# Mixer projections and gates as single fp32 products of unsplit weights

## The chip, the cores and the metric

The kernel runs on one core of a Trainium2 chip. The metric is the device time of one execution in microseconds (us). One execution is also recorded by the hardware profiler, with every instruction on its engine: PE (TensorE, the matmuls; PEld are its weight loads), DVE (VectorE), ACT (ScalarE), POOL (GpSimd) and SP, which issues most DMA transfers from one queue in order.

## The reference

Two layers of a diffusion transformer block on 256 context and 256 latent tokens, each token a vector of 1024. All is in fp32. The part around the change is the mixer: one normed input `h` is projected by one wide weight into the inputs of three mixers and a gate for each, and the gated outputs are merged.

```python
for layer in range(DEPTH):                       # DEPTH = 2
    x = ffn_half(x, ...); ctx = ffn_half(ctx, ...)
    h  = norm_modulate(x, ...);  hc = norm_modulate(ctx, ...)
    mix, mix_c = hybrid_mixer(h, hc, not last, w_in[layer], ...)
    x = x + m[5] * mix
    x = ffn_half(x, ...)                         # the context too, unless last

def hybrid_mixer(h, hc, need_ctx_out, w_in, ...):
    proj = h @ w_in                              # and proj_c = hc @ w_in
    u, k, v, f = split_cols(proj[..., :CTX_STATE_COLS], sizes)
    q = proj[..., CTX_STATE_COLS:MIX_COLS]
    y_s5  = s5_mixer(u, ...)                     # state space model, two directions
    y_att = gqa_mixer(q, k, v, ...)              # attention over context and latent
    y_rw  = rwkv7_mixer(f, ...)                  # RWKV-7 recurrence, two directions
    g_s5, g_att, g_rw = split(sigmoid(proj[..., MIX_COLS:]), 3)
    return (g_s5*(y_s5 @ w_br_s5) + g_att*(y_att @ w_br_att) + g_rw*(y_rw @ w_br_rwkv)) @ w_out
```

In the last layer only the latent tokens need an output, so the gates, the queries and some of `f` are computed for 256 tokens there.

## The kernel before

Activations lie with features on the partitions, as tiles of [128, 8, 512]: 8 blocks of 128 features by 512 tokens. A product of one 128x128 weight block with 256 tokens is called a product of 256 columns below; a [128x1024] strip of weights is 8 such blocks.

Precision is kept by splitting: `wsplit` (L904) copies an fp32 weight tile to a float32r tile `hi` on ACT (L906) and subtracts it on DVE or POOL (L907) to get `lo`; the FFN has its own `wunit` (L909). The norm writes its output split too, into `K.hhi` and `K.hlo` (`norm`, L1066). `mm3` (L921) then adds three float32r matmuls into one bank: hi by hi, hi by lo, lo by hi.

`mixers` (L1245) emits one layer's mixers. First the entry: two strips of RWKV's features (`pf` of t = 2, 3). Then `kknorm`, whose first matmuls write `kkss` (L110). Then the operations named in `SEQ`, in that order: `f` strips of RWKV's features (`pf`), `u` strips of S5's input (`pu`), `k` key/values (`pkv`), `q` queries (`pq`), `g4` or `g8` gates (`pg`). Those behind the bar are emitted inside `rw.run(between)`, between the two directions of the first half of RWKV's tokens. The rest of the 24 gates follow the attention. RWKV's own chain is: `prep`, which for each half of the tokens, direction and part computes `ZL`, `BK` and on PE `it` (L208), masked into `AM`; `solve_a`, which stores `AM` in DRAM (`Ad`), loads its diagonal blocks as `G`, inverts them in 15 short steps on DVE (`stmp` L240, `S` L241), and moves `S` through DRAM (`Sd`) into `D`; `solve_b`, which transposes `D` to `T` (DVE, L252) and starts the matmuls `pv` (L256); then the loop over chunks. S5 and attention (units of `atp`, `atP`, `ato`; L869 to L885) are emitted behind; then the merge: products `pb` with the gates, and `po` with `w_out`.

Code order is not engine order: the Tile framework's scheduler orders each engine's instructions when the kernel is built, from its own estimates and priorities; on the chip each engine runs its list in order and waits by semaphores. Weight tiles come from pools with few buffers: `wr` (3 of 256 KB), `gh` and `gl` (2 halves each) in the mixers.

Of the kernel before, what the change touches and what calls it, by code (L numbers as in the profile page):

```python
# [928 lines left out]
def dense(K,name,src,hhi,hlo,n0,nk=8,eng=None,alt=False,fill=False,cut=False,half=False,big=False):  # L929

    ps=mm(K,name,alt=alt); m=K.FM[n0>0]
    if cut: prods(K,ps,name,src,nk,hhi,hlo,n0,eng,half,big=big)
    else:
        for k in range(nk):
            j=slice(k%4*128,k%4*128+128)
            if k%4==0: hi,lo=wunit(K,src[:,k*128:(k+4)*128],512,eng)
            K.lastp=mm3(K.nc,ps[:,n0:],hi[:,j],lo[:,j],hhi[:,k,n0:],hlo[:,k,n0:],k==0,k==nk-1)
    return ps
# [14 lines left out]
def prods(K,ps,name,src,nk,hhi,hlo,n0,eng=None,half=False,z=512,big=False):  # L953

    w=K.NG if half else z-n0
    if big:
        for k in range(nk):
            if k%4==0:
                raw=K.rw.tile([128,512],F32,name=f"wr{name}{k}",tag="g2",bufs=K.TB[3])
                sp=K.rw.tile([128,2,512],F32R,name=f"wp{name}{k}",tag="f4",bufs=K.TB[0])  # L960
                K.nc.sync.dma_start(raw,src[:,k*128:k*128+512])
                wsplit(K,sp[:,0],sp[:,1],raw,eng)
            j=slice(k%4*128,k%4*128+128)
            for c in range(n0,z,w):
# [101 lines left out]
def norm(K,L,sub,n0,tag):  # L1066
# [24 lines left out]
    for h,v,s in hv:  # L1091
        for k in range(8):
          with K.tc.high_priority(offset=K.NQ) if v and n0==0 else nullcontext():
# [4 lines left out]
              if k%K.NP==K.NP-1:  # L1098
# [58 lines left out]
def build(tc,I,O,depth=DEPTH):  # L1157
    K=NS(); K.nc=nc=tc.nc; DQ=0; K.dq=nc.scalar if DQ&1 else nc.sync; K.S5C=2; K.FO=(6,0,1); K.FO2=(4,5,7); K.KV=0; K.FA=((),()); K.RG=2; K.EB=(); K.UP=(4,1); K.sq=nc.scalar if DQ&2 else nc.sync; K.rq=nc.scalar if DQ&4 else nc.sync; K.I=I; K.BG=(12,12); K.PO=4; K.SM=2; K.NPR=75; K.NQ=0; K.ATP=(1,1); K.GQ=((4,0),(0,0)); K.KP=9; K.PW=0; K.CA=6; K.NP=3; K.nu=0; K.after=None; K.hold=None; K.ADR=3; K.WB=3; K.TB=(4,4,10,4,4); K.ATT=3; K.ATQ=2; K.GA=(10,20); K.GB=(3,2); K.S5B=3; K.S5U=K.S5B; K.S5T=6; K.ATB=(2,1,1,1); K.fin=False; K.GTB=1; K.QB=(2,2); K.SP=2; K.GHB=2; K.NG=256; K.GP=2; K.HW=0; K.ORD='s s s s s g10 k u g3 u g3 u g3 u;s s s s s g20 k u g2 u'.replace('_',' ').split(';'); K.tc=tc; K.hop=None; K.FM=(6,9); K.GF=(24,24); K.HP=(5000,5000); K.HS=(0,0); K.HK=(0,0); K.ATT=5
# [9 lines left out]
    with es:  # L1168
# [9 lines left out]
        K.hhi=K.hp.tile([128,8,512],F32R,name="hhi"); K.hlo=K.hp.tile([128,8,512],F32R,name="hlo")  # L1178
# [63 lines left out]
v='v'  # L1242
def ix(v,L): return v[L] if isinstance(v,tuple) else v['v']

def mixers(tc,K,L,last):  # L1245
# [12 lines left out]
    with tc.tile_pool(name="mc",bufs=1) as mc, tc.tile_pool(name="q0",bufs=1) as q0, tc.tile_pool(name="prm",bufs=1) as K.prm, \  # L1258
# [194 lines left out]
```

## Time and profile before

| | |
|---|---|
| device time, median of 3 runs | 2347.73 us (2344.19 to 2353.74) |
| profiled execution: its own time / its span | 2359.33 us / 2357.6 us |
| mean granted clock of TensorE | 0.953 |
| PE, DVE, ACT, POOL busy | 95%, 69%, 41%, 26% |
| layer 0: `kkss`, first `pv`, second batch of `pv`, `po` | 466.8, 641.6, 724.0, 950.0 us |
| layer 1: the same | 1768.3, 1919.5, 1980.5, 2121.4 us |

The span is the time from the first to the last instruction in the trace. Busy time counts an engine's instructions with their overlaps taken out; a matmul's record is longer than the distance to the next one, since matmuls are pipelined. The last two lines are read from the starts of those instructions in the trace; they cut each layer's mixers into the three stretches that the prediction works with.

### The profile page before, as it was taken

Reading aid. Unit: us, or ns where it says so; the run is one execution under the profiler, and the core shown is the slowest. Engines: PE = TensorE matmul, PEld = TensorE weight load, DVE = VectorE, ACT = ScalarE, POOL = GpSimd, SP = SyncE. Lnnn points to the kernel's source line nnn. Section 1 sums busy time; section 2 is a strip of 40 time slices with the busy share of each in tenths; the row PEclk is TensorE's granted clock in tenths of the full one; section 3 lists DMA queues with packets and bytes.
Section 4 is the critical chain, followed back from the end, with each engine's and each line's share of the span. In section 5 each row is a group of like instructions: output and inputs, shape, how many; then the busy total and the mean of one; then the engine's idle time right before and its main releaser. Section 6 shows DMA issues by size and latency. Waiting matters only on the chain.

```text
span 2357.6 us, 40039 instructions
## 1 busy us (share of the span) xinstructions
PE 2242.8 (95%) x14438; PEld 1929.4 (82%) x14438; DVE 1623.2 (69%) x3202; ACT 973.7 (41%) x2005; POOL 607.1 (26%) x726
## 2 busy tenths in 40 slices
PE   7999889988999999899999999999999899998999
PEld 3888668866789889788888888888887688888999
DVE  7895889588855677886457575546557965687655
ACT  4333333433344544443233344334334325565554
POOL 5016660155422233600000002513013533331000
PEclk8999989998869999999999999999999877999999
DMA  7575566334422454545445436546424542365664
GB/s 254 165 225 171 182 214 219 121 119 144 123 82 76 138 163 143 185 141 184 123 143 182 126 131 206 171 155 215 138 65 131 150 126 85 94 194 184 178 188 130
DMA packets 222715, 363.40 MB, mean 154 GB/s; under 512 B 53554, under 2 KB 93618, under 8 KB 222388
## 3 DMA queue, kind: packets, MB, share of 16 engines
q1 hardware_dynamic: 220500, 360.09, 48.3%
q8 instruction: 113, 1.85, 0.3%
q10 hardware_dynamic: 2016, 0.76, 0.1%
q14 instruction: 86, 0.70, 0.1%
HBM read 320.90 MB, written 39.86 MB: 153 GB/s over the span
## 4 chain that ended last, share of the span: by engine, by line
PE 79%; DVE 10%; issue 4%; DMA 3%; POOL 2%; ACT 1%; SPq 1%; DVEq 0%; ACTq 0%; POOLq 0%
PE p L922 17%; PE p L924 17%; PE p L923 16%; PE pg L924 3%; PE pg L922 3%; PE pg L923 3%; DVE s L995 1%; PE pS L261 1%; PE pv L256 1%; PE pq L923 1%; PE po L922 1%; PE po L924 1%; PE po L923 1%; PE pq L922 1%; PE it L208 1%
## 5 line engine op out<-in xcount | busy, mean ns | idle before, releaser
L917 ACT ACTIVATE wh<-wr 128x512 fp32r<-128x512 f32 (+1 forms) x568 | 348.1, 619 | 666.3 <-PE p L923 578.1
L918 DVE TENSOR_TENSOR wl<-wr,wh 128x512 fp32r<-128x512 f32 (+1 forms) x568 | 407.3, 721 | 306.3 <-ACT wh L917 275.1
L922 PE MATMUL p<-hhi,wh 128*128 128x512 f32 (+1 forms) x1440 | 516.6, 363 | 4.7 <-ACT wh L917 3.6
L923 PE MATMUL p<-hlo,wh 128*128 128x512 f32 (+1 forms) x1440 | 518.6, 361 | 1.5 <-DVE hlo L1104 0.9
L924 PE MATMUL p<-hhi,wl 128*128 128x512 f32 (+1 forms) x1440 | 518.6, 361 | 0.6 <-DVE wl L918 0.6
L922 PEld LDWEIGHTS p<-hhi,wh 128*128 128x128 f32 x1440 | 273.2, 191 | 46.7 <-ACT wh L917 4.3
L923 PEld LDWEIGHTS p<-hlo,wh 128*128 128x128 f32 x1440 | 274.2, 190 | 42.9 <-DVE hlo L1104 1.8
L924 PEld LDWEIGHTS p<-hhi,wl 128*128 128x128 f32 x1440 | 274.0, 190 | 42.4 <-DVE wl L918 1.4
L995 DVE SCALAR_TENSOR_TENSOR s<-ad,cb 128x1024 f32<-128x1024 f32 x224 | 286.3, 1280 | 2.9
L924 PE MATMUL p<-ghi,wl 128*128 128x512 f32 (+1 forms) x704 | 248.3, 353 | 0.0
L922 PE MATMUL p<-ghi,wh 128*128 128x512 f32 (+1 forms) x704 | 248.0, 353 | 0.0
L923 PE MATMUL p<-glo,wh 128*128 128x512 f32 (+1 forms) x704 | 247.9, 353 | 0.0
L924 PE MATMUL pg<-hhi,glpg 128*128 128x256 f32 x512 | 157.9, 309 | 11.0 <-DVE glpg L907 9.0
L922 PE MATMUL pg<-hhi,ghpg 128*128 128x256 f32 x512 | 155.5, 304 | 0.3 <-ACT ghpg L906 0.3
L923 PE MATMUL pg<-hlo,ghpg 128*128 128x256 f32 x512 | 152.0, 297 | 0.0
L924 PEld LDWEIGHTS p<-ghi,wl 128*128 128x128 f32 x704 | 133.0, 189 | 18.2 <-issue 0.2
L923 PEld LDWEIGHTS p<-glo,wh 128*128 128x128 f32 x704 | 133.0, 189 | 18.1
L922 PEld LDWEIGHTS p<-ghi,wh 128*128 128x128 f32 x704 | 133.0, 189 | 17.9
L906 ACT ACTIVATE ghpg<-wrpg 128x256 fp32r<-128x256 f32 x176 | 72.3, 414 | 125.3 <-PE pg L923 102.9
L924 PEld LDWEIGHTS pg<-hhi,glpg 128*128 128x128 f32 x512 | 104.6, 205 | 18.8 <-DVE glpg L907 10.9
L907 POOL TENSOR_TENSOR glpg<-wrpg,ghpg 128x256 fp32r<-128x256 f32 x88 | 70.8, 808 | 180.8 <-ACT ghpg L906 168.7
L922 PEld LDWEIGHTS pg<-hhi,ghpg 128*128 128x128 f32 x512 | 104.8, 205 | 6.3 <-ACT ghpg L906 0.5
(722 smaller groups left out, 4325.5 us busy)
## 6 DMA issues: line engine op xcount, KB each, us to landing
wr<-w SPq DMA_DIRECT2D x480, 256.0 KB
ad<-w_ada SPq DMA_DIRECT2D x138, 512.0 KB
wrpg<-w_g SPq DMA_DIRECT2D x96, 256.0 KB
wr<-w SPq DMA_DIRECT2D x64, 192.0 KB
s5tab<-s5tabd SPq DMA_DIRECT2D x16, 640.0 KB
s5tabd<-s5tb SPq DMA_DIRECT2D x16, 384.0 KB
wrpf<-w_f SPq DMA_DIRECT2D x24, 256.0 KB
gd<-gt SPq DMA_DIRECT2D x24, 256.0 KB
```

Source lines behind the costliest of these rows:

```text
L208: nc.tensor.matmul(pi[:,c,:],BK[R,c].rearrange("p j b -> p (j b)"),s.ZL[par][R,hf,dq,c,o],start=True,stop=True)
L256: for m in range(16): h=nc.tensor.matmul(pv[R,m,:],AMv[H,m,c:c+32],T[H,m,:],start=True,stop=True)
L261: for m in range(16): h=nc.tensor.matmul(pS[R,m,:],VT[R,m,:],D[R,m,:],start=True,stop=True)
L906: K.nc.scalar.activation(hi,raw,AF.Copy)
L907: (K.nc.gpsimd if eng=='pool' else K.nc.vector).tensor_sub(lo,raw,hi.bitcast(F32))
L917: nc.scalar.activation(hi[:,0:n],raw,AF.Copy)
L918: (nc.gpsimd if eng=='pool' or i<=K.PW else nc.vector).tensor_sub(lo[:,0:n],raw,hi[:,0:n].bitcast(F32))
L922: nc.tensor.matmul(ps,lhi,rhi,start=start,stop=False)
L923: nc.tensor.matmul(ps,lhi,rlo,start=False,stop=False)
L924: return nc.tensor.matmul(ps,llo,rhi,start=False,stop=stop).ins
L995: nc.vector.scalar_tensor_tensor(j,raw,1.0,K.cb[:,v,:],op0=ALU.mult,op1=ALU.mult,accum_out=K.M[L][:,v,ct:ct+1])
```

## The change

All products of `pf`, `pu`, `pkv`, `pq` and `pg` become single fp32 matmuls of the fp32 weight tile with an fp32 `h`. The norm ahead of the mixers writes only `K.h`, in the memory of `hlo` (one ACT instruction in place of ACT and DVE or POOL). All these products have 256 columns; before, `pu` and most `pf` had 512. Weight tiles alternate between two tags (`wr` 3 and `gs` 2 buffers). Four of the eight `po` keep the split, through `prods3`. `hlo` is allocated anew for the merge, since `h` lay in its place; in the last layer the split halves of the mixers' outputs lie side by side in `hhi`. The FFNs, attention, `pb` and `po` stay products of three parts.

```diff
-def prods(K,ps,name,src,nk,hhi,hlo,n0,eng=None,half=False,z=512,big=False):
...
-        if k%2==0:
-            hi=K.wr.tile([128,256],F32R,name=f"gh{name}{k}",tag="gh",bufs=K.GHB)
-            lo=K.wr.tile([128,256],F32R,name=f"gl{name}{k}",tag="gl",bufs=K.GHB)
-            wsplit(K,hi,lo,raw[:,k%4*128:k%4*128+256],eng)
-        h=hi[:,k%2*128:k%2*128+128]; l=lo[:,k%2*128:k%2*128+128]
-        for c in range(n0,z,w):
-            s=slice(c,c+w)
-            mm3(K.nc,ps[:,s],h,l,hhi[:,k,s],hlo[:,k,s],k==0 and c==n0,k==nk-1 and c+w==z)
+def wraw(K,name):
+    K.npr+=1; tag,b=(("wr",K.WB),("gs",2))[K.npr%5%2]
+    return K.wr.tile([128,512],F32,name=f"wr{name}",tag=tag,bufs=b)
...
+def prods(K,ps,name,src,nk,n0,half=False):
+
+    w=K.NG if half else 512-n0
+    for k in range(nk):
+        if k%4==0:
+            raw=wraw(K,f"{name}{k}")
+            with K.tc.issue_after(K.hold) if K.hold else nullcontext(): K.nc.sync.dma_start(raw,src[:,k*128:k*128+512])
+        j=slice(k%4*128,k%4*128+128)
+        for c in range(n0,512,w):
+            K.nc.tensor.matmul(ps[:,c:c+w],raw[:,j],K.h[:,k,c:c+w],start=k==0 and c==n0,stop=k==nk-1 and c+w==512)
...
-def norm(K,L,sub,n0,tag):
+def norm(K,L,sub,n0,tag,f32=False):
...
-              if k%K.NP==K.NP-1:
+              if f32: nc.scalar.activation(K.h[:,k,s],t,AF.Identity,bias=b)
+              elif k%K.NP==K.NP-1:
...
+            K.h=K.hp.tile([128,8,512],F32,name=f"h{L}",tag="hlo")
+            norm(K,L,1,0,f"m{L}",True)
...
-                hi=K.wr.tile([128,256],F32R,name=f"gh{nm}{L}{tps[0]}{k}",tag="gh",bufs=K.GHB); l=K.wr.tile([128,256],F32R,name=f"gl{nm}{L}{tps[0]}{k}",tag="gl",bufs=K.GHB)
-                wsplit(K,hi,l,raw[:,k%2*256:k%2*256+256],'pool' if k%K.KP==K.KP-1 else None)
...
-                        mm3(nc,b[:,i],K.hhi[:,k,c],K.hlo[:,k,c],hi,l,k==0 and i==0,k==7 and i==1)
+                        nc.tensor.matmul(b[:,i],K.h[:,k,c],raw[:,k%2*256:k%2*256+256],start=k==0 and i==0,stop=k==7 and i==1)
...
-            pf=[(mm(K,f"pf{L}{t}e",alt=t%2==1),wunits(K,I['w_f'][L,t],8)) for t in (2,3)]
-            units(K,pf,K.hhi,K.hlo)
+            for c in (slice(0,256),slice(256,512)):
+                for ps,ws in pf:
+                    for k in range(8): nc.tensor.matmul(ps[:,c],ws[k//4][:,k%4*128:k%4*128+128],K.h[:,k,c],start=k==0,stop=k==7)
```

How the scheduler's order moves, at three places. In the rows a name's number tells one tile from another; `x4` is four rows alike.

The first place is PE in layer 0, in the first half of RWKV's tokens, where direction 1's `it` is computed. Before:

```order
L924 MATMUL pkv_4744<-ghkv_4813,hlo 128x256
L922 MATMUL pkv_4744<-ghkv_4813,hhi 128x256
L923 MATMUL pkv_4744<-glkv_4814,hhi 128x256
L924 MATMUL pkv_4744<-ghkv_4813,hlo 128x256
L208 MATMUL it_5606<-ZL_4032,BK_5601 128x128 x4
L922 MATMUL pkv_4744<-ghkv_4823,hhi 128x256
L208 MATMUL it_5613<-ZL_4033,BK_5601 128x128 x4
L922 MATMUL pkv_4836<-ghkv_4839,hhi 128x256
L923 MATMUL pkv_4744<-glkv_4824,hhi 128x256
L924 MATMUL pkv_4744<-ghkv_4823,hlo 128x256
L922 MATMUL pkv_4744<-ghkv_4823,hhi 128x256
L923 MATMUL pkv_4744<-glkv_4824,hhi 128x256
```

After:

```order
L1295 MATMUL pq_4661<-wrq_4668,h_3866 128x256 x4
L1295 MATMUL pq_4661<-wrq_4674,h_3866 128x256 x4
L1295 MATMUL pq_4661<-wrq_4680,h_3866 128x256 x4
L1295 MATMUL pq_4689<-wrq_4690,h_3866 128x256 x4
L1295 MATMUL pq_4689<-wrq_4696,h_3866 128x256 x4
L1295 MATMUL pq_4689<-wrq_4702,h_3866 128x256 x4
L1295 MATMUL pq_4689<-wrq_4708,h_3866 128x256 x4
L208 MATMUL it_4739<-ZL_4013,BK_4734 128x128 x4
L208 MATMUL it_4746<-ZL_4014,BK_4734 128x128 x4
L975 MATMUL pg_7115<-h_3866,wrpg_7116 128x256 x8
L975 MATMUL pg_7115<-h_3866,wrpg_7126 128x256 x4
L221 MATMUL bt_4754<-ident,BK_4734 128x128 x4
```

Before, `it` of direction 1 stood among the products of `pkv`; now all of `between()`'s `pkv`, the four gates and the queries stand ahead of it.

The second place is PE at the end of layer 0's attention, in the last unit. Before, from its first instruction on:

```order
L857 MATMUL atm_7858<-ident,atmh_7299 128x128
L869 MATMUL atp_7866<-atqs_7661,atkh_7293 128x512
L870 MATMUL atp_7866<-atqs_7661,atkl_7294 128x512
L924 MATMUL pg_9049<-hhi,glpg_9103 128x256
L922 MATMUL pg_9049<-hhi,ghpg_9102 128x256
L922 MATMUL pb03e_8934<-es_8845,ee_8929 128x512
L923 MATMUL pb03e_8934<-es_8845,ee_8929 128x512
L924 MATMUL pb03e_8934<-es_8845,ee_8929 128x512
L922 MATMUL pb03e_8934<-es_8845,ee_8929 128x512
L923 MATMUL pb03e_8934<-es_8845,ee_8929 128x512
L924 MATMUL pb03e_8934<-es_8845,ee_8929 128x512
L923 MATMUL pg_9049<-hlo,ghpg_9102 128x256
```

After, in the same unit, a few steps in:

```order
L869 MATMUL atp_7025<-atqs_6794,atkh_6426 128x512
L870 MATMUL atp_7025<-atqs_6794,atkl_6427 128x512
L871 MATMUL atp_7025<-atmT_6433,atsel_6438 128x512
L878 MATMUL ato_6998<-atph_7005,atvh_6428 128x512
L879 MATMUL ato_6998<-atph_7005,atvl_6429 128x512
L880 MATMUL ato_6998<-atpl_7006,atvh_6428 128x512
L869 MATMUL atp_7038<-atqs_6794,atkh_6426 128x512
L870 MATMUL atp_7038<-atqs_6794,atkl_6427 128x512
L871 MATMUL atp_7038<-atmT_6433,atsel_6438 128x512
L878 MATMUL ato_6998<-atph_7018,atvh_6428 128x512
```

Before, gate products and `pb` stood between the unit's matmuls; now its matmuls follow each other, and all 24 gates lie ahead of the unit.

The third place is DVE in layer 0, right behind `kkst`, the instruction that reads `kkss`. Before:

```order
L907 TENSOR_TENSOR glpf_4341<-wrpf_4328,ghpf_4340 128x256
L116 COPY kkrb_4195<-kkrn_4193 128x1024
L907 TENSOR_TENSOR glpf_4361<-wrpf_4358,ghpf_4360 128x256
L907 TENSOR_TENSOR glpf_4371<-wrpf_4358,ghpf_4370 128x256
L121 TENSOR_TENSOR kkn_4176<-kkn_4176,kkb_0_4197 128x512
L121 TENSOR_TENSOR kkn_4176<-kkn_4176,kkb_1_4203 128x512
L87 SCALAR_TENSOR_TENSOR wal_4031<-pf_4305,rwder_4021,ls_6_4353 128x512
L907 TENSOR_TENSOR glpf_4383<-wrpf_4380,ghpf_4382 128x256
L907 TENSOR_TENSOR glpf_4393<-wrpf_4380,ghpf_4392 128x256
L687 TENSOR_TENSOR s5ra_6992<-s5v_6987,s5tab_6983 128x512
L688 TENSOR_TENSOR s5rb_6993<-s5v_6987,s5tab_6983 128x512
L907 TENSOR_TENSOR glpf_4413<-wrpf_4410,ghpf_4412 128x256
```

After:

```order
L116 COPY kkrb_4096<-kkrn_4094 128x1024
L121 TENSOR_TENSOR kkn_4077<-kkn_4077,kkb_0_4098 128x512
L121 TENSOR_TENSOR kkn_4077<-kkn_4077,kkb_1_4104 128x512
L87 SCALAR_TENSOR_TENSOR wal_4012<-pf_4158,rwder_4002,ls_6_4182 128x512
L87 SCALAR_TENSOR_TENSOR r_4207<-pf_4186,rwder_4002,ls_0_4211 128x512
L168 TENSOR_SCALAR th_4245<-th_4245 128x256
L181 SCALAR_TENSOR_TENSOR T_4279<-ta_4246,kkn_4077 128x256
L169 SCALAR_TENSOR_TENSOR th_4245<-c_rst_3994,th_4245 128x256
L87 SCALAR_TENSOR_TENSOR r_4207<-pf_4214,rwder_4002,ls_1_4238 128x512
L168 TENSOR_SCALAR th_4251<-th_4251 128x256
```

The subtracts of L907 are gone, and `prep`'s rows (`r`, `th`, `T`) have moved up.

## Rows read from the trace of the kernel before

**Rows 1.** The page: span, busy time by engine, the chain by engine, one group.

```profile
span 2357.6 us, 40039 instructions
...
PE 2242.8 (95%) x14438; PEld 1929.4 (82%) x14438; DVE 1623.2 (69%) x3202; ACT 973.7 (41%) x2005; POOL 607.1 (26%) x726
...
PE 79%; DVE 10%; issue 4%; DMA 3%; POOL 2%; ACT 1%; SPq 1%; DVEq 0%; ACTq 0%; POOLq 0%
...
L907 POOL TENSOR_TENSOR glpg<-wrpg,ghpg 128x256 fp32r<-128x256 f32 x88 | 70.8, 808 | 180.8 <-ACT ghpg L906 168.7
```

**Rows 2.** Busy time by stretch: A, B, C of layer 0, then of layer 1.

```profile
core 0: us, PE busy (x) PEld busy (x) DVE busy (x) ACT busy (x) POOL busy (x), PEclk, DMA share, GB/s
466.80:641.60 174.80, 149.57 (x861) 121.74 (x859) 144.43 (x284) 64.74 (x143) 86.31 (x106) 0.92 0.44 131
641.60:724.00 82.40, 82.06 (x911) 72.82 (x911) 43.92 (x110) 36.99 (x89) 18.45 (x23) 0.75 0.31 90
724.00:950.00 226.00, 226.00 (x2063) 205.41 (x2063) 153.27 (x337) 108.26 (x217) 69.41 (x67) 0.99 0.40 130
1768.30:1919.50 151.20, 129.79 (x779) 110.92 (x777) 128.24 (x272) 59.93 (x143) 67.52 (x93) 0.88 0.49 143
1919.50:1980.50 61.00, 59.69 (x682) 51.85 (x682) 30.30 (x74) 26.55 (x67) 15.76 (x24) 0.75 0.33 96
1980.50:2121.40 140.90, 136.48 (x1446) 124.07 (x1446) 97.18 (x185) 81.25 (x181) 48.99 (x54) 0.92 0.43 131
```

**Rows 3.** The same windows for L907 alone: A of both layers, and the sum.

```profile
466.80:641.60 174.80, 31.44 (x57) 5.92 (x8) 0.92 0.44 131
...
1768.30:1919.50 151.20, 27.58 (x58) 9.94 (x12) 0.88 0.49 143
...
sum 836.30, DVE 138.32 POOL 76.79; mean DVE 23.05 POOL 12.80
```

**Rows 4.** Timeline of PE: start, duration, instruction; fp32r of 512 and 256 columns, fp32.

```profile
400.17 0.39 PE L923 MATMUL p<-glo,wh 128*128 128x512 f32 x1
400.39 0.39 PE L924 MATMUL p<-ghi,wl 128*128 128x512 f32 x1
...
628.88 0.28 PE L923 MATMUL pg<-hlo,ghpg 128*128 128x256 f32 x1
629.00 0.28 PE L924 MATMUL pg<-hhi,glpg 128*128 128x256 f32 x1
...
1821.73 1.02 PE L95 MATMUL gg<-sg,gup 128*128 128x256 f32 x4
```

**Rows 5.** Groups by tile: count, then duration in ns, min/median/max.

```profile
L95 PE MATMUL gg<-sg,gup x8: 377/484/592, 544.2 to 1822.4; 128*128 128x512 f32 x4, 128*128 128x256 f32 x4
...
L240 DVE TENSOR_TENSOR stmp<-S,G x60: 160/209/740, 578.9 to 1923.6; 128x15 f32<-128x15 f32 x8, 128x28 f32<-128x28 f32 x8, 128x39 f32<-128x39 f32 x8, 128x48 f32<-128x48 f32 x8
```

**Rows 6.** Timeline: last `it`, first solve step, store of S; both layers.

```profile
561.71 0.48 PE L208 MATMUL it<-ZL,BK 64*128 64x128 f32 x2
...
578.86 0.16 DVE L240 TENSOR_TENSOR stmp<-S,G 128x15 f32<-128x15 f32 x1
...
630.18 0.44 SPq L242 DMA_DIRECT2D Sd<-S  x1
...
1835.33 1.60 PE L208 MATMUL it<-ZL,BK 64*128 64x64 f32 x16
...
1851.69 0.17 DVE L240 TENSOR_TENSOR stmp<-S,G 128x15 f32<-128x15 f32 x1
...
1901.71 0.38 SPq L242 DMA_DIRECT2D Sd<-S  x1
```

**Rows 7.** Timeline of attention: one step's exponential and the next, a division.

```profile
2077.11 0.60 ACT L873 ACTIVATE atP<-atp 128x512 f32<-128x512 f32 x1 [0.58 <-PE atp L871]
...
2079.21 0.59 ACT L873 ACTIVATE atP<-atp 128x512 f32<-128x512 f32 x1
...
905.05 3.35 DVE L884 RECIPROCAL atdn<-atdn 128x512 f32<-128x512 f32 x1 [4.42 <-ACT atdn L883]
```

More of the change, by code (lines that the diff above doesn't have):

```diff
@@ L927, in mm, with dense @@
     return K.pa(list(shape),name) if alt else K.mm(shape,name)
-def dense(K,name,src,hhi,hlo,n0,nk=8,eng=None,alt=False,fill=False,cut=False,half=False,big=False):
+def dense(K,name,src,hhi,hlo,n0,nk=8,eng=None,alt=False):
     ps=mm(K,name,alt=alt); m=K.FM[n0>0]
[L932 to L937, printed above, removed]
+    for k in range(nk):
+        j=slice(k%4*128,k%4*128+128)
+        if k%4==0: hi,lo=wunit(K,src[:,k*128:(k+4)*128],512,eng)
+        K.lastp=mm3(K.nc,ps[:,n0:],hi[:,j],lo[:,j],hhi[:,k,n0-512:],hlo[:,k,n0-512:],k==0,k==nk-1)
     return ps
@@ L1283, in mixers, with mixp @@
         rw=Rwkv(K,L,W,last); rw.emit=lambda hf,o: ysplit(6,8,o) if last else nc.sync.dma_start(K.yd[:,6:8,hf*256:hf*256+256],o)
-        feat=lambda t: rw.feat(t,dense(K,f"pf{L}{t}",I["w_f"][L,t],K.hhi,K.hlo,256 if last and t in (0,1,7) else 0,alt=t in ix(K.FA,L),cut=True))
+        def mixp(name,src,n,alt=False,half=False):
+            ps=mm(K,name,alt=alt); prods(K,ps,name,src,8,n,half); return ps
+        feat=lambda t: rw.feat(t,mixp(f"pf{L}{t}",I["w_f"][L,t],256 if last and t in (0,1,7) else 0,alt=t in ix(K.FA,L),half=True))
         def proj(nm,w,dst,tps):
@@ L1300, in proj, with gate @@
                 nc.scalar.activation(g,b,AF.Copy); K.dq.dma_start(dst(tp),g)
-        def gate(j,big=False):
+        def gate(j):
             g=q0.tile([128,512],F32,name=f"gt{L}{j}",tag="gt",bufs=K.GTB)
-            ps=dense(K,f"pg{L}{j}",I['w_g'][L,j],K.hhi,K.hlo,n0,eng='pool' if K.GP and j%K.GP==1 else None,cut=True,half=True,big=big)
+            ps=mixp(f"pg{L}{j}",I['w_g'][L,j],n0,half=True)
             nc.scalar.activation(g[:,n0:],ps[:,n0:],AF.Tanh,scale=0.5)
@@ L1319, in op @@
             if c=='f': feat(int(o[1]))
-            elif c=='u': t=int(o[1]); s5_u(K,L,t,dense(K,f"pu{L}{t}",I['w_u'][L,t],K.hhi,K.hlo,0,cut=True),q0)
+            elif c=='u': t=int(o[1]); s5_u(K,L,t,mixp(f"pu{L}{t}",I['w_u'][L,t],0,half=True),q0)
             elif c=='g': gates(int(o[1:])); ng[0]+=int(o[1:])
@@ L1345, in mixers @@
         gates(16-ng[0])
[L1347 removed]
+        if last: yk=lambda i: (K.hhi[:,i,0:256],K.hhi[:,i,256:512])
         else:
@@ L1371, in mixers @@
                 nc.scalar.activation(v[:,0],yr,AF.Copy); nc.vector.tensor_sub(v[:,1],yr,v[:,0].bitcast(F32))
+        K.hlo=K.hp.tile([128,8,512],F32R,name=f"hlo{L}",tag="hlo")
+        K.mx=(K.hlo[:,:,0:256],K.hlo[:,:,256:512]) if last else (K.hhi,K.hlo)
         for m in range(8):
@@ L1395, in merge @@
                 if m<7: continue
-                units(K,todo,K.hhi,K.hlo)
+                units(K,todo,*K.mx)
                 for j in range(len(todo)): resid(K,L,5,8-len(todo)+j,todo[j][0],n0)
                 continue
-            else: ps=dense(K,f"po{L}{m}",I['w_out'][L,m],K.hhi,K.hlo,n0,cut=m<K.PO,alt=m%2==1)
+            elif m<K.PO: ps=mm(K,f"po{L}{m}",alt=m%2==1); prods3(K,ps,f"po{L}{m}",I['w_out'][L,m],8,*K.mx,n0)
+            else: ps=dense(K,f"po{L}{m}",I['w_out'][L,m],*K.mx,n0,alt=m%2==1)
             resid(K,L,5,m,ps,n0)
```

54 lines of the change are left out of this document (25 added, 29 removed).

## The prediction

> **What bounds the kernel now.** I read the page first. PE is busy 95% of the span and the chain that ended last lies on it for 79%, so the program looks like one long queue of matmuls [rows 1]. But the change touches only the mixers, and an average over the program says little of them. So I cut each layer's mixers at three landmarks that exist in both versions: `kkss` (the key norm, right after the entry), the first and the second batch of `pv` (the RWKV triangular solve, once per half of the tokens) and the first `po` (w_out). That gives stretches A (`kkss` to first `pv`), B (to the second `pv`) and C (to `po`), 836 us in both layers together, and I read each engine's busy time and the clock in each [rows 2].
>
> The reader should see that A is not C. In C of layer 0 PE is busy for all of its 226 us at a clock of 0.99. In A, DVE is busy for 144 of 175 us and 128 of 151 us, with PE at 150 and 130, and "busy" flatters PE there: in A of layer 0 the order has 214 of the products that change (counted in 256 columns), and by the spacing of rows (below) they are only 75 us of work. The rest of PE's rows in A, summed from the order with the spacing of their own form, is 41 us. So 116 us of work took 175 us; in layer 1 it is 90 of 151, in B 54 of 82 and 38 of 61. C of layer 0 holds 216 us of work in 226, C of layer 1 117 in 141. A waits for DVE and for the RWKV chain; C of layer 0 waits for PE.
>
> Who fills DVE in A? The split's subtract (L907) is 31 us of it in layer 0 and 28 us in layer 1, of 138 us of DVE and 77 us of POOL in the six stretches [rows 3].
>
> **The price on PE.** Rows follow each other at 0.12 us for an fp32r product of 256 columns (628.88 to 629.00) and 0.22 to 0.23 us for 512 (400.17 to 400.39) [rows 4]; measured over longer runs of rows I use 0.119 and 0.227. One product in three parts is thus 0.357 us at 256 columns and 0.681 at 512. The trace of before has no large fp32 matmul with 128-row weights except `gg`: four instructions of 256 columns and four of 512 give 16 records, two each, and four records of 256 columns take 1.02 us where the shortest `gg` record is 0.377 [rows 4, 5]. The difference over three steps is 0.215 us a record, 0.43 us a product. The two layers hold 640 and 392 products of 128x128 by 256 columns, 1032. Before, 104 pairs of them (`pf` 72, `pu` 32) went as 512 columns: 104 x 0.681 + 824 x 0.357 = 365 us. After: 1032 x 0.43 = 444 us. PE gets **79 us more work**. The bounds of the price: nothing less than two records of the fp32r kind (2 x 0.119 = 0.24 us), nothing in the rows above 0.43.
>
> A rule speaks against the change. The Trainium skill, "FP8 and Floating Point Precision", section TensorE Precision Notes, says that true FP32 takes 4 passes through the array. By that rule, four passes for three, an estimate is a third more than 365 us, +122 us. The trace agrees that fp32 is the dearer one, but has it at 0.43 for 0.357, a fifth more; the sum goes by the trace.
>
> **What goes away.** All splits of `pf`, `pu`, `pkv`, `pq` and `pg`: by the order 268 fewer DVE, 344 fewer ACT and 100 fewer POOL rows, mostly L906 and L907. Those on DVE in A count most. By the order, DVE has 256 rows between `kkst` and the first transpose T in layer 0 before, and 119 after; at the mean durations of their groups 148 and 66 us. In layer 1, 130 and 54 us. Only about a third of that drop is removed work; the rest is S5 steps that moved behind. By the same count B's DVE goes from 30 to 54 us and from 20 to 60 us. In C of layer 0 it does not pile up: 342 us in the layer's three stretches before, less some 64 of splits, less 66 and 54, leave 158 us. So **DVE no longer bounds A, and PE does**: the scheduler puts products there, 341 against 214 in layer 0 and 265 against 166 in layer 1. B has 102 against 77 and 66 against 53, and C keeps 144 against 293 and 8 against 117. PE's work by stretch after is: A 147 + 22 = 169, B 44 + 36 = 80, C 62 + 113 = 175; layer 1: 114 + 18 = 132, 28 + 30 = 58, 3 + 77 = 81.
>
> **Stretch by stretch.** *A.* Two paths end it. One is PE's sum, 169 and 132. The other is the chain: in after all of `between()`'s products (key/values, four or eight gates, queries) stand ahead of direction 1's `it`, as the rows of the order show; PE's sum up to there is 139 us in layer 0 and 104 in layer 1. From the last `it` of before the path ran 17 us to the first solve step, then 30 short steps spread over 51 us because DVE ran other rows between them, then 11 us from the store of S to `pv` [rows 6]; layer 1: 16, 50 and 18 us. Alone, 30 steps of 0.21 us [rows 5] with the gap between two are some 8 us, and with the 17 and 11 that stand around them 36; with layer 1's 16 and 18, 42. DVE has 47 rows, 18 us, left in that place, so I take 42 us in both layers, in place of 80 and 84: A = 139 + 42 = 181 (**+6**) and 104 + 42 = 146 (**-5**). *B.* 80 us of PE plus 4 for the steps that wait for the chain, 84 (**+2**); in layer 1 DVE 60 and PE 58, with some waiting for each other, 68 (**+7**). *C, layer 0.* PE's sum falls from 216 to 175. But the gates were also the filler of attention. Now they end earlier, and the last unit is bare, as the order shows. Nothing hides a step there: exponential to next exponential 2.1 us of ACT and DVE against 6 fp32r products, 1.4 us; the division at the end waits 4.4 us and takes 3.35 [rows 7]. The bare stall is between 0 (C = 175) and 51 (no gain); eight steps of 0.7, the division with its neighbours some 10, and the end of the RWKV chain as much again make 25: C = 200 (**-26**). *C, layer 1.* PE has 81 us of work, so the chain bounds: about 63 us of RWKV loop and first unit and some 62 us to `po` with less filler between; 125 (**-16**), bounds 81 and 141. *Entry* (`pf` of t = 2, 3, in both layers): 53 products of 0.43 stand ahead of `kkss` after, 22.8 us, and 55 of 0.357 before, 19.6: **+3** each. `po`, `pb` and the FFNs keep their work; the paired splits of four `po` I take at nothing, since the chain on DVE there is under PE's queue.
>
> Sum: +6 +2 -26 -5 +7 -16 +6 = **-26**, and the norm, which writes one tile where it wrote two and loses a subtract pass behind its last step in both halves (POOL's subtract of 256 columns takes 0.81 us [rows 1]), -3 for two layers: -29 us. The profiled execution took 2359.3 us, 11.6 above the median of the runs, 2347.7; I take the same 29 off the median: **2318 us**, 1.25% faster.
>
> The transfers keep their bytes. The tightest is A of layer 1: 99 more products, four to a tile of 256 KB, are 25 tiles, 6.5 MB on top of 143 GB/s x 151 us = 21.6 MB, a DMA share of some 0.66 in place of 0.49 [rows 2]. I count them as hidden.
>
> **The rivals.** A change of 0.5%, 12 us, is about what can be told from none.
> *The stalls vanish.* A dense order on PE keeps the clock up, and solve and attention fit under it. Floor: all six stretches at PE's sum (B of layer 1 at DVE's 60): 697 against 836, with the entries -133. Halfway between my sum and the floor, -80: 2268. For it: C of layer 0 was within 10 us of its sum. Against: layer 1 has too little filler. Chance 0.15.
> *The price eats the gain.* A keeps half of its former excess over PE's sum (58 and 61 us) instead of 12 and 14: A takes 198 and 162, 17 and 16 more than forecast, and the rest is as forecast: +4, 2352, within 0.5%. Chance 0.18.
> *The RWKV chain is late: slower.* If the solve's steps wait among other DVE rows as before, the path from direction 1's `it` to `pv` stays 80 and 84 us, and A = 219 and 188. That is +44 and +37 where I had +6 and -5: the total is -29 + 80 = +51, 2399. It decides from 56 us on that path in both layers on (nothing gained). Against it: few DVE rows stand there now. Chance 0.10.
> *PE was the bound throughout.* Then the 79 us come on top: 2427. Against it: the 59 us of A that are not PE's work. Chance 0.05. By the passes of the Trainium skill's page the same case would be an estimated 2470; no row here gives that.
>
> **Chances and range.** Forecast 0.52, and with the vanishing stalls 0.67 for faster; same 0.18; slower 0.15. The range leaves out the slower cases and the lower part of the first rival: 2268 to 2360. The likeliest case alone is 2300 to 2336.
>
> **What would show it.** Products of 128x256 fp32 in two records 0.215 us apart; DVE in A at 70 to 100 us; first `pv` 181 and 146 us after `kkss`; C at 200 and 125 us; a last attention unit in C of layer 0 with idle PE. Wrong would be: records further apart or at the lower clock in A; a solve still spread over 50 us; C of layer 1 as long as before.

## The result: slower by 3.1%

The changed kernel takes 2427.77 us (median of 4, 2423.69 to 2428.96) against 2350.73 us of before beside it: ratio 1.0311, 95% interval 1.0283 to 1.034. The forecast was 2318 us. From the page of the changed kernel's profile, the rows that answer to [rows 1]:

```profile
span 2426.9 us, 37368 instructions
...
PE 2308.3 (95%) x13718; PEld 1941.1 (80%) x13718; DVE 1482.0 (61%) x2934; ACT 845.1 (35%) x1661; POOL 512.2 (21%) x626
...
PE 79%; DVE 9%; DMA 3%; issue 3%; ACT 2%; POOL 2%; SPq 0%; DVEq 0%; ACTq 0%; POOLq 0%
```

DVE lost 141 us of busy time, ACT 129, POOL 95, and none of it came back as a shorter span: PE gained 66 us of busy time. The windows A, B and C of both layers of the changed kernel, as in [rows 2]:

```profile
467.20:662.10 194.90, 185.12 (x882) 156.46 (x880) 66.58 (x132) 33.70 (x64) 38.55 (x57) 0.95 0.43 130
662.10:761.80 99.70, 98.24 (x1012) 85.35 (x1012) 61.75 (x129) 23.32 (x51) 37.96 (x45) 0.91 0.34 100
761.80:995.30 233.50, 210.53 (x1488) 162.66 (x1488) 137.06 (x247) 88.97 (x171) 46.76 (x46) 0.90 0.32 101
1825.10:1968.60 143.50, 143.50 (x723) 120.81 (x722) 49.15 (x119) 30.46 (x67) 28.57 (x44) 1.00 0.55 164
1968.60:2054.30 85.70, 84.00 (x817) 73.40 (x816) 60.17 (x123) 18.32 (x42) 30.04 (x42) 0.82 0.44 123
2054.30:2193.10 138.80, 114.14 (x1119) 88.85 (x1117) 89.97 (x184) 62.48 (x129) 31.42 (x36) 0.82 0.26 79
```

Such a row can be split into three parts: PE's **idle** time (length less PE busy), time **lost to the clock** (length times one less the granted clock), and the rest, PE's **work** at full clock. Idle and lost together are the stalls below. The split is rough. A busy PE need not be at its peak, and idle time at a low clock is counted twice. After, e3, e5, e6, e14, e15 and e16 run the very same matmuls, and by this split they have between 715 and 795 us of work. So a difference of a few tens of us between two rows of the last two columns proves little; times and lengths are firmer. A of layer 1 after the change is the pure case: 143.5 us long, 143.5 busy, clock 1.00. C of layer 0 is the other: 23 us idle and 23 lost, where before had 0 and 2.

In us, summed over the six stretches, with the device time of every run of this study and its ratio to the runs of before made beside it (their median lies between 2350.5 and 2359.5 us):

| kernel | time | ratio (95%) | stretches | work | stalls |
|---|---|---|---|---|---|
| before | 2350.7 | 1 | 836 | 702 | 134 |
| after | 2427.8 | 1.031 (1.028 to 1.034) | 896 | 753 | 143 |
| e1 price off | 2329.7 | 0.989 (0.987 to 0.992) | 806 | 664 | 143 |
| e2 price a third | 2226.0 | 0.946 (0.942 to 0.950) | 707 | 431 | 276 |
| e3 gates held | 2486.5 | 1.057 (1.053 to 1.061) | 944 | 715 | 229 |
| e4 before, 4th part | 2421.2 | 1.030 (1.026 to 1.034) | 907 | 822 | 85 |
| e5 late | 2446.7 | 1.041 (1.038 to 1.044) | 909 | 752 | 157 |
| e6 late and held | 2463.8 | 1.047 (1.044 to 1.050) | 925 | 738 | 187 |
| e7 before, one part | 2277.7 | 0.968 (0.965 to 0.971) | 754 | 453 | 301 |
| e8 before, fp32 | 2383.3 | 1.013 (1.008 to 1.017) | 854 | 781 | 74 |
| e9 after, plus bf16 | 2492.4 | 1.059 (1.055 to 1.064) | 960 | 866 | 93 |
| e10 ACT copy, 4 | 2424.3 | 1.032 (1.027 to 1.036) | 892 | 773 | 119 |
| e11 before, fp32, no subtract | 2370.9 | 1.010 (1.006 to 1.014) | 834 | 770 | 63 |
| e12 after, paced | 2399.3 | 1.020 (1.016 to 1.024) | 866 | 773 | 93 |
| e13 ACT copy, 2 | 2369.2 | 1.006 (1.004 to 1.009) | 837 | 776 | 61 |
| e14 after, 2 tiles | 2368.4 | 1.007 (1.005 to 1.010) | 834 | 768 | 65 |
| e15 after, 3 tiles | 2435.3 | 1.035 (1.033 to 1.038) | 901 | 760 | 141 |
| e16 after, 2 halves | 2432.8 | 1.032 (1.029 to 1.035) | 914 | 795 | 120 |

So of the 60 us that the stretches gained, 51 are work and 9 stalls by this split. The stalls mostly changed place: A from 79 to 20 us in the two layers, B from 37 to 28, C from 18 to 96. The other 9 us of the span lie mostly between `po` and the next FFN of layer 0, 58 before and 67 after.

### The profile page after: what moved, and what is told of

It is laid out like the page before. It is cut to its first block, busy times and chain, and to the rows that moved or that the text cites. A ratio compares the mean times of both kernels' runs of the same rounds, so it can differ in the third digit from the quotient of the medians.

```text
span 2426.9 us, 37368 instructions
## 1 busy us (share of the span) xinstructions
PE 2308.3 (95%) x13718; PEld 1941.1 (80%) x13718; DVE 1482.0 (61%) x2934; ACT 845.1 (35%) x1661; POOL 512.2 (21%) x626
## 4 chain that ended last, share of the span: by engine, by line
PE 79%; DVE 9%; DMA 3%; issue 3%; ACT 2%; POOL 2%; SPq 0%; DVEq 0%; ACTq 0%; POOLq 0%
PE p L922 16%; PE p L923 16%; PE p L924 16%; PE pg L975 9%; PE pf L975 3%; PE pq L1295 2%; PE it L208 1%; DVE s L991 1%; PE pu L975 1%; PE pkv L1295 1%; PE pv L256 1%; PE pS L261 1%; DVE atdn L884 1%; PE s5v L683 1%; PE s5y L710 1%
## 5 line engine op out<-in xcount | busy, mean ns | idle before, releaser
L918 DVE TENSOR_TENSOR wl<-wr,wh 128x512 fp32r<-128x512 f32 (+1 forms) x560 | 400.9, 719 | 303.2 <-ACT wh L917 274.9
L975 PE MATMUL pg<-h,wrpg 128*128 128x256 f32 x1152 | 285.5, 396 | 0.8 <-DMA wrpg<-w_g 0.8
L975 PEld LDWEIGHTS pg<-h,wrpg 128*128 128x128 f32 x1152 | 217.4, 197 | 33.3 <-issue 3.7
L1133 DVE TENSOR_TENSOR s<-s,p 128x512 f32<-128x512 f32 (+1 forms) x88 | 54.5, 619 | 63.8 <-PE p L924 62.3
L213 DVE TENSOR_TENSOR AM<-it,c_mask 64x512 f32<-64x512 f32 (+1 forms) x32 | 19.8, 618 | 114.5 <-PE it L208 114.4
L975 PE MATMUL pf<-h,wrpf 128*128 128x256 f32 x336 | 78.5, 388 | 0.0
L1109 DVE SCALAR_TENSOR_TENSOR xT<-p,M,xT 128x256 f32<-128x256 f32 x106 | 47.4, 479 | 46.4 <-PE p L924 46.3
```

Source lines behind the costliest of these rows:

```text
L918: (nc.gpsimd if eng=='pool' or i<=K.PW else nc.vector).tensor_sub(lo[:,0:n],raw,hi[:,0:n].bitcast(F32))
L975: K.nc.tensor.matmul(ps[:,c:c+w],raw[:,j],K.h[:,k,c:c+w],start=k==0 and c==n0,stop=k==nk-1 and c+w==512)
L1109: nc.vector.scalar_tensor_tensor(K.xT[:,m,s],(ps[1-v] if isinstance(ps,tuple) else ps)[:,s],g,K.xT[:,m,s],op0=ALU.mult,op1=ALU.add)
L1133: nc.vector.tensor_mul(s[:,n0:],s[:,n0:],p3[:,n0:])
```

## The experiments

**The price.** Two kernels without splits and with a cheaper product, `n` = 3 and 1; one with the change and a bf16 matmul on top; and two on the kernel before, with a fourth and with only one part.

```diff
-            K.nc.tensor.matmul(ps[:,c:c+w],raw[:,j],K.h[:,k,c:c+w],...)
+    hi=lambda a: a.bitcast(mybir.dt.bfloat16)[:,1::2]
+    for i in range(n): K.nc.tensor.matmul(ps,hi(w),hi(x),...)     # e1: n=3, e2: n=1
...
+    K.nc.tensor.matmul(ps,w,x,...)                                # e9
+    K.nc.tensor.matmul(ps,hi(w),hi(x),...)
...
+    nc.tensor.matmul(ps,llo,rlo,start=start,stop=False)           # e4, ahead of mm3
...
+    nc.tensor.matmul(ps,lhi,rhi,start=start,stop=stop)            # e7, in place of mm3
```

> The changed kernel with each fp32 product of the mixers replaced by three bf16 products of the upper halves of the same words (another result, three times a product of less precision): no splits, as after, but PE pays about 0.36 us a product in place of 0.43, as before the change. Price theory (the dearer products are the loss, the stalls only changed place): 1032 x 0.07 = 75 us come back, 2350 us. Order theory (the gates have moved ahead into the first stretch and left the last one without filler; the price would be hidden otherwise): the last stretch of each layer stays as long as after (234 and 139 us), only the first stretch gets shorter, by at most 25 and 20 us: 2385 to 2400 us.

> As the run with three bf16 products, but one bf16 product in place of three (another result, of less precision): PE pays some 0.12 us a product, 320 us less work than after. It shows what the other engines and the chains leave when PE is nearly free. Price theory: a large part comes back, about 200 us, 2220 us, and the stretches end at their chains (first stretch about 110 us). Order theory: the last stretches have no filler at all and stay near 190 and 130 us; 2260 us or more.

> The kernel before with a fourth float32r matmul, lo by lo, in each changed product: splits, buffers and DVE's work stay, PE gets 104 x 0.227 + 824 x 0.119 = 122 us more work. If PE's work counts everywhere: 2347 + 122 = 2470 us. If it counts only outside the first stretch, where before had 59 and 61 us of PE time that was not its work: the 45 us that fall there are hidden, 2425 us.

> The kernel before with only hi by hi of the three parts in each changed product (less precision): all splits stay on ACT, DVE and POOL, PE pays 0.12 us a product, as in the run with one bf16 product and no splits (2226 us). If the splits on DVE bound the first stretch, as the prediction had it, then the first stretch stays near 175 and 151 us and the time is 2270 us or more. If the RWKV chain bounds it and the splits lie beside it, the time is within 15 us of 2226.

> The changed kernel with one bf16 matmul more in each product (its sum is added: another result): PE gets 1032 x 0.1135 = 117 us more work, no split comes back. If PE's work counts in full from here on, as it did from 0.34 to 0.43 us a product (98 us for 93): 2428 + 117 = 2545 us. If the stalls of after (some 160 us idle or at the lower clock in both layers) take up a part of it, as before's did of the fourth part (68 for 122): 2495 us.

Timeline of PE, of the changed kernel and then of e1 (start, duration, instruction, records), and e1's windows of A in both layers:

```profile
539.67 3.40 PE L975 MATMUL pf<-h,wrpf 128*128 128x256 f32 x15
```

```profile
558.75 4.24 PE L953 MATMUL pg<-h,wrpg 128*128 128x256 bf16 x36
```

```profile
462.70:647.10 184.40, 169.71 (x1338) 137.06 (x1337) 93.38 (x174) 39.62 (x76) 57.73 (x82) 0.94 0.50 154
1757.40:1926.90 169.50, 164.79 (x1297) 134.42 (x1296) 92.12 (x189) 39.55 (x88) 52.02 (x77) 0.95 0.61 187
```

Fourteen steps in 3.40 less some 0.39 us are 0.215 us a record, 0.43 a product: the forecast's price. The bf16 record takes 0.113 us, so e1's product costs 0.34, less than expected of it. From there to after, 1032 products by 0.09 us are 93 us of work, and the time rises by 98: the price counts in full, as the price theory had it. (The time is below what either theory named, 2350 or 2385 to 2400, and the last stretches, 206 and 122 us, did not stay as the order theory had them.) Yet before with a fourth part (e4) paid only 67 of 122 us, as its second branch had it, and after with one more matmul (e9) only 65 of 117: by the split the stalls took the rest (134 to 85, 143 to 93). So whether PE's work costs its full length depends on the stalls there are, and on the order that fills them.

e1 also shows what removing the splits was worth at about before's price: 24 us less than before beside it (2353.8), of which 14 are its cheaper product if that counts in full (351 us against 365). That leaves **about 10 us**, and the stalls stay, 143 against 134. A did not get shorter: 184 and 170 us where before had 175 and 151, with DVE busy for only 93 and 92 us of it. e2 and e7 fit that. With PE nearly free, A still takes 153 and 141 us without a single split (e2, whose price theory had the time right, 2220, but A at some 110), 171 and 146 with all of them (e7). What is left there without splits are the chains of RWKV and S5 and the products still in A; no run separates these. The splits cost 52 us in all between e2 and e7, but only 18 and 5 in A; e7 stands as expected of splits that bind, but the binding shows when PE is nearly free, not at before's price.

**Moving the products by hand.** Order edges on PE (`issue_after`) put the gates behind later instructions (e3, which also takes four gates out of each layer's `between()`), or `between()`'s queries and gates are emitted behind direction 1 (e5), or both, with the last ten and six gates held (e6).

```diff
+            with tc.issue_after(h.ins) if h is not None else nullcontext(): prods(K,ps,f"pg{L}{j}",...)   # e3, e6
...
-        between()
-        s.prep(h1); s.solve_a(0)
+        between(0)                                                # e5, e6: f4 f5 f7 k-0 k-1
+        s.prep(h1); s.solve_a(0)
+        between(1)                                                # gates and queries
```

> The changed kernel with the gates' matmuls queued on PE behind later instructions: no gate between RWKV's two directions in layer 0 and four in place of eight in layer 1, six behind the first pv, four behind the second, the rest behind the score matmuls of the attention units. By the order the first stretch holds 203 and 179 of the changed products in place of 341 and 265, the last 320 and 112 in place of 144 and 8. Price theory: PE's sum is the same, the time stays within 15 us of 2428. Order theory: the last stretch has its filler back and the first one is shorter by the gates taken out: first 165 and 135, second 80 and 65, last 250 and 145 us, in all some 45 us less: 2380 us.

> The changed kernel with the queries and the four or eight gates of between() emitted behind direction 1's prep and the solve, instead of ahead of them; features and key/values stay ahead. By the order the first stretch of layer 0 then holds 219 of the changed products, as before the change (214), not 341. Queue theory (the chain is late because its matmuls stand behind 300 dense products on PE): direction 1's `it` comes 27 to 40 us earlier in layer 0, about 20 in layer 1, and both batches of pv with it: 2380 us. Price theory (PE's sum counts, wherever it stands): within 15 us of 2428.

> As the run with queries and gates behind direction 1, and in addition the last ten gates of layer 0 and the last six of layer 1 queued on PE behind the score matmuls of successive attention units, so that the last stretch keeps filler to its end. Filler theory: the idle and half-clock time of the last stretches (some 45 and 50 us after the change) halves, 30 to 40 us less than the run without the hold: 2345 us. Price theory: no change against that run, within 15 us.

All three are slower than after, by 59, 19 and 36 us, and none came out as one of its theories had it: e3 and, by a little, e5 lie above what even the price theory allowed, and e6 takes 17 us more than e5 where the filler theory had 30 to 40 less. In e5 the first `pv` comes 133 and 116 us after `kkss` instead of 195 and 144, so the chain is earlier by 62 and 28 us, and the time is longer: the **queue theory falls**. In e3 A is 199 us long at a clock of 0.81, with 37 us idle: gates taken out of A left PE gaps there, and C of layer 1 was no better filled (30 idle, 32 lost). In e6 the last gates stand 33 and 32 us ahead of `po`, and C takes 280 and 177 us, longer than in e5 (262 and 175). So "more filler in C" by coarse holds falls as well: each shifted the stalls.

**The lead.** What the splits may also have done is to keep the products back: PE could read most weights only from two half tiles (`gh`, `gl`), where after can have five whole tiles of weights ready. How far the products may run ahead of the rest in this way is called the lead. e8 keeps before's splits and waits, but does one fp32 matmul a product; e11 drops the subtract from it; e10, e12 and e13 put copies into the changed kernel; e14 to e16 change nothing in it but the weight buffers.

```diff
-    mm3(K.nc,ps[:,s],h,l,hhi[:,k,s],hlo[:,k,s],...)
+    nc.tensor.matmul(ps,(llo if odd else lhi).bitcast(F32),rhi.bitcast(F32),...)   # e8; e11: lhi alone, no subtract
...
+    t=K.wr.tile([128,256],F32,name=f"gc{name}",tag="gs",bufs=4)   # e10; e13: 2 buffers of its own
+    K.nc.scalar.activation(t,raw,AF.Copy)
+    (K.nc.gpsimd if eng=='pool' else K.nc.vector).tensor_mul(u,t,K.one...)   # e12: a second copy u, by DVE or POOL
...
-    K.npr+=1; tag,b=(("wr",K.WB),("gs",2))[K.npr%5%2]
-    return K.wr.tile([128,512],F32,name=f"wr{name}",tag=tag,bufs=b)
+    K.npr+=1; return K.wr.tile([128,512],F32,name=f"wr{name}",tag="gs",bufs=2)     # e14; e15: "wr", 3; e16: [128,256], 2
```

> The kernel before, its splits still made and waited for, with one fp32 matmul a product in place of three float32r: of the high part of the weight for even blocks, of the low part for odd ones, by the high part of the input (another result). PE pays the 0.43 us of the change (79 us more than before) while products still come at the pace of the splits. If the price alone explains the loss: 2353 + 75 = 2428 us, as after. If the removal of the splits is itself a part of the loss (products run ahead into the first stretch and no longer fill the last one): by the slope of the run with a fourth part (68 us for 122), 2353 + 79 x 0.56 = 2397 us.

> The changed kernel with each half weight tile copied by ACT (fp32 to fp32, four half buffers in place of the two whole ones) before PE reads the copy: no subtract, but products come at ACT's pace with 1 to 2 tiles of lead. Pace theory: gates and queries no longer run ahead, the stalls of the last stretches (46 and 50 us) shrink, 2400 us or less. Price theory: 2428 us within 15.

> As the kernel before with one fp32 matmul a product, but the subtract of the changed products left out and both blocks taken from the part that ACT writes, two half tiles ahead (another result): DVE and POOL are freed as in the change, PE pays 0.43 us a product, and by the order the queries still stand one by one between the solve's steps and the last four gates at the end. Lead theory (what decides is how far the products may run ahead, not who is busy): 2383 us as with the subtracts, within 15. If the freed DVE is itself what moves the order and the time, as in the change: 2420 us or more.

> The changed kernel with each half weight tile copied by ACT and then again by DVE or POOL (the same engines as the split's subtract) before PE reads it, two half tiles ahead; the result is that of the changed kernel. By the order the queries stand between the solve's steps and the gates reach the attention units again, as before the change. Lead theory: the 45 us between after and the fp32 products at the splits' pace come back, 2385 us. If something else of the change costs them (one tile of h in place of two, 256 columns in place of 512, the buffers): 2428 us, or more by the work added.

> The run with ACT's copies once more, with two half buffers for the copies in place of four; the result is that of the changed kernel. Lead theory: the time falls from 2424 to about 2375 to 2390 us, since products can then stand only one tile ahead, as in the kernel before. If it was the fp32 h, the 256 columns or the paired splits of po, it stays at 2424 us.

> The changed kernel with one line changed: two buffers of 256 KB for its weight tiles in place of five (no copies, no added work; the result is that of the changed kernel). Lead theory: by the order the queries stand one by one between the solve's steps and the gates reach the attention again, so the time falls to 2380 to 2395 us although the transfers have less lead. If the lead is not the cause: 2428 us or more, since PE then waits for weights too.

> The changed kernel with three buffers of 256 KB for its weight tiles in place of five; the result is that of the changed kernel. By the order the queries stand in one piece ahead of the first pv, as after the change, but the gates somewhat later. Lead theory: between the run with two buffers and after, 2400 to 2420 us. Otherwise 2428 us.

> The changed kernel with two buffers of 128 KB for its weights (half tiles, twice as many transfers), half the lead of the run with two whole tiles; the result is that of the changed kernel. By the order the gates reach further back still (the last five beside the last products ahead of po). Lead theory with a lower limit: less lead still spreads the filler, but a half tile holds only 0.9 to 1.7 us of PE's work while its transfer takes longer, so PE now waits for weights: 2400 us or more, above the 2368 us of two whole tiles. If only the spread of the products mattered: 2368 us or less.

e8 pays the same price as after and takes 44 us less: price alone is not the loss. e11 shows that it isn't the busy DVE that helps, since without the subtracts it is no slower (2371 against 2383 us, with intervals that overlap). e10, with four half buffers, is after again, where its pace theory had 2400 or less; e13, with two, is 55 us faster. Only the tags and counts of these buffers differ between the two; the split halves of four `po` share them in both. And e14, one line, gives 59 us with no added work. Both e13 and e14 come out a little below what the lead theory expected. They keep the fp32 `h`, the 256 columns and the paired splits of `po`, so none of these makes the 55 to 59 us. e14's windows, to be laid beside those of after:

```profile
465.40:600.60 135.20, 128.25 (x666) 106.26 (x664) 81.96 (x157) 29.29 (x57) 55.09 (x71) 0.99 0.47 147
600.60:727.40 126.80, 124.83 (x1116) 102.34 (x1116) 64.85 (x141) 34.30 (x75) 35.26 (x47) 0.99 0.38 117
727.40:951.50 224.10, 219.24 (x1610) 181.59 (x1610) 120.18 (x213) 83.53 (x153) 33.66 (x30) 0.96 0.34 112
1782.20:1929.20 147.00, 136.32 (x729) 113.83 (x728) 90.92 (x192) 34.09 (x74) 57.80 (x80) 0.95 0.50 152
1929.20:1989.50 60.30, 57.57 (x674) 46.91 (x673) 26.68 (x84) 20.01 (x48) 14.29 (x21) 0.97 0.47 136
1989.50:2129.60 140.10, 131.41 (x1268) 108.75 (x1267) 79.63 (x149) 57.57 (x115) 22.10 (x21) 0.94 0.35 110
```

No clock is below 0.94, and C of layer 0 has 5 us idle in place of 23. The 63 us that the six stretches lose lie in A and B (524 to 469 us over both layers); C is 8 us shorter, but holds far more gate products. PE's gate records (two to a product) in C, layer 0 and layer 1, with their first and last start, first after, then e14:

```profile
L975 PE MATMUL pg<-h,wrpg x289: 377/379/795, 761.5 to 871.6; 128*128 128x256 f32 x145
L975 PE MATMUL pg<-h,wrpg x16: 379/634/795, 2063.4 to 2075.9; 128*128 128x256 f32 x16
```

```profile
L974 PE MATMUL pg<-h,wrpg x439: 377/379/634, 727.1 to 900.0; 128*128 128x256 f32 x147
L974 PE MATMUL pg<-h,wrpg x176: 377/379/795, 1994.4 to 2078.0; 128*128 128x256 f32 x176
```

So in e14 some 155 more gate products, 67 us at 0.43, fit into a C that is no longer: they stand where PE had stalls. The last one starts 51 and 52 us ahead of `po`, after the change 124 and 117; in e13 28 and 36, in e10 124 and 104. PE's order in layer 0's solve shows the same for the queries, first e14, then the changed kernel. A `pS` row is a run of the solve's tiny matmuls, which wait for results of DVE and ACT; in e14 four products of a query stand between two such runs, in after all queries are long done:

```
L261 MATMUL pS_5039<-D_4807,T_4971 32x32 x7
L1294 MATMUL pq_4661<-wrq_4668,h_3866 128x256 x4
L261 MATMUL pS_5039<-D_4807,T_4971 32x32 x9
L1294 MATMUL pq_4661<-wrq_4674,h_3866 128x256 x4
```

```
L208 MATMUL it_4957<-ZL_4014,BK_4945 128x128 x4
L261 MATMUL pS_5039<-D_4807,T_4971 32x32 x52
L975 MATMUL pg_7211<-h_3866,wrpg_7222 128x256 x2
```

Three tiles (e15) already let the products run ahead and are no better than five, not the middle that was expected; its weights also share another tag (`wr`, with those of `po`) than e14's (`gs`), and no run tells the tag from the number. Two half tiles (e16) are too few; its waits of PE, the longest in sum (engine, line, what for: us in total, times, longest):

```profile
PE pg L974 <- DMA wrpg<-w_g: 23.4, 24, 4.3
PE pf L974 <- DMA wrpf<-w_f: 14.8, 12, 2.3
```

There PE waits for weights: the five kinds of changed products wait 57 us in all, with two whole tiles 10 (`pg` once, for 2.4 us). So from five tiles down to two less lead was better in the end, though not step by step, and with two half tiles, whose transfers are also half as large, it was worse. The count of tiles is not the whole of it: e10's four half buffers are two tiles' worth too, and it is as slow as after. There a freed buffer is filled by ACT out of three loaded tiles, in e14 by a new transfer, and no run takes this apart. e12, paced by two copies, got only 28 of the 45 us, less than its lead theory had.

## Why the prediction was wrong

**The price of the product: right.** It is 0.43 us as forecast, and PE's work in the stretches grew by 51 us by the split (forecast 64). The Trainium skill's rule ("FP8 and Floating Point Precision", TensorE Precision Notes: 4 passes for true FP32) comes near: 0.43 us are 3.6 times the 0.119 of one fp32r part. Four passes for three parts would be a third more, which is an estimate from that rule; the trace has a fifth, and the trace decides.

**The stalls that the change was to win back: wrong, the step that failed.** The forecast took 205 us of the stretches for stalls (*"A waits for DVE and for the RWKV chain"*), and let them fall by 96, to 109, once the splits were gone. Measured they rose by 9, from 134 to 143, and e1 shows the splits' removal to be worth about 10 us. The changes of length, in us, layer 0 and layer 1:

| stretch | forecast | measured |
|---|---|---|
| A | +6, -5 | +20, -8 |
| B | +2, +7 | +17, +25 |
| C | -26, -16 | +8, -2 |

The misses add up to 92 us. Of these 58 are PE's sums, too small in every stretch: *"the rest of PE's rows in A, summed from the order ... is 41 us"* and its like gave 631 us of work before and 695 after, where the windows hold 702 and 753 by the split. So 71 us of before that the forecast took for stalls, to be won back, were not. Where they lie was not taken apart. The other 34 us are stalls after the change that it priced too low, 143 in place of 109. A had 20 (forecast 26) and B 28 (forecast 14), but C had 96 where 69 were forecast: *"some 10, and ... as much again make 25"* for layer 0 was 46, and in layer 1, where 44 were forecast, it was 50. What was won in A was lost in C. The forecast saw that the gates leave C, but priced the bare rest too low.

**DVE in A** fell to 67 and 49 us, below the 70 to 100 named, and it no longer bounded A, as forecast; A still took 195 and 143.5, where 181 and 146 were forecast. Rows of the changed kernel for the chain, layer 0 and then layer 1: the last `it`, the first and the last step of the solve, the first `pv`.

```profile
628.36 1.16 PE L208 MATMUL it<-ZL,BK 64*128 64x128 f32 x8
...
637.45 0.17 DVE L240 TENSOR_TENSOR stmp<-S,G 128x15 f32<-128x15 f32 x1 [6.49 <-DMA G<-Ad]
...
652.15 0.18 DVE L241 TENSOR_TENSOR S<-S,stmp 128x15 f32<-128x15 f32 x1
...
662.08 0.62 PE L256 MATMUL pv<-T,AM 16*32 16x32 f32 x14
...
1938.03 1.10 PE L208 MATMUL it<-ZL,BK 64*128 64x64 f32 x8
...
1948.11 0.17 DVE L240 TENSOR_TENSOR stmp<-S,G 128x15 f32<-128x15 f32 x1 [2.27 <-DMA G<-Ad]
...
1959.14 0.18 DVE L241 TENSOR_TENSOR S<-S,stmp 128x15 f32<-128x15 f32 x1
...
1968.65 0.56 PE L256 MATMUL pv<-T,AM 16*32 16x32 f32 x12
```

The solve's steps take 15 and 11 us in place of some 50, and the path from the last `it` to `pv` 34 and 31 us, better than the 42 forecast. But the last `it` starts 161 and 113 us after `kkss`, where PE's sum had 139 and 104. So layer 0 is 14 us worse, and in layer 1 two errors cancel: the number is right by luck. **B** took 100 and 86 in place of 84 and 68: half 1's `prep`, ahead of the first `pv` before, lies in B after (its first `it` at 663.6 us, the first `pv` at 662.1). **C** took 234 and 139 in place of 200 and 125. The bare attention unit went at 2.0 us a step (forecast 2.1); timeline of ACT in the changed kernel:

```profile
963.04 0.60 ACT L873 ACTIVATE atP<-atp 128x512 f32<-128x512 f32 x1 [0.76 <-DVE atpl L876]
...
965.06 0.60 ACT L873 ACTIVATE atP<-atp 128x512 f32<-128x512 f32 x1 [0.76 <-DVE atpl L876]
```

**The rivals.** The number came out as in the last one, which took the 79 us on top of everything (2427), with a chance of 0.05. That match is luck. Its mechanism, no stall to win, is not what happened: at the same price e8, e11, e13 and e14 are 44 to 59 us faster than after (stalls of 61 to 74 in place of 143), but with the free run of the products none of it was won. The late RWKV chain (0.10) did not occur: its condition was a path of 80 and 84 us, and it is 34 and 31. Direction 1's `it` is late (148 us after `kkss` in layer 0, before 85), as the forecast itself had it (139), and e5, where the first `pv` comes 62 and 28 us earlier and the time is longer, shows that this alone isn't what costs.

**The cause, then.** The price is 79 us of PE work; with two tiles of lead the stalls absorb most of it (e14: some 17 us slower than before). With five, the products run ahead, PE is full in A and bare in C, and nothing is absorbed: 77 us. That the weight buffers decide is shown by e13 against e10 and by e14 against after. That they do it by the place of the gates and queries in PE's order is read from the orders and windows. It is not shown by itself: a buffer count changes both the order that the scheduler builds and the waits on the chip, and the moves by hand (e3, e5, e6), which also changed the place, gained nothing. Open stay also the 9 us behind `po`: in that window DVE is busy for 58 of 67 us after and 46 of 58 before, but e14 has 70 us there too, and no run took this apart. No version that computes the whole result at full precision beat before.

## What to carry to other kernels

When a step that feeds an engine is removed, ask what it held back: the scheduler may then place independent work early, and the work that filled the gaps of later chains is gone. Before counting a gap as winnable, split the window's own length into idle, lost clock and work, and compare it with the sum from the order; here the sum of spacings was 71 of 702 us too small. A buffer count can act as a pacing knob and is worth trying in both directions: here 5, 3, 2 and 1 tiles' worth gave 2428, 2435, 2368 and 2433 us, so a step in one direction alone says little.

## What the runs showed of the hardware

The granted clock was 1.00, its upper level, over the 143.5 us of A in layer 1 after the change, in which PE was busy throughout; it was 0.973 for all of e14 against 0.953 of before. A bf16 record of 256 columns took 0.113 us (the 36 records above), an fp32r one 0.119, an fp32 one 0.215, two of them to a product. In a stretch of e1 where the granted clock was 0.51, near its lower level, the bf16 records stand 0.21 us apart:

```profile
1941.66 4.56 PE L953 MATMUL pg<-h,wrpg 128*128 128x256 bf16 x21
```
